# One pool of eight PSUM banks for every product, in place of three banks for dense tiles and five for the rest, with new leads

## The chip, the cores and the metric

The kernel runs on one core of a Trainium2 chip. The metric is device microseconds of one execution, as a median of several runs; less is faster. TensorE (PE in the profile) multiplies matrices and writes only to PSUM, an accumulator memory of eight banks, each of 128 partitions by 512 fp32 numbers here. VectorE (DVE) and ScalarE (ACT) read the banks and write their results to SBUF. GpSimd (POOL) helps with elementwise work in SBUF. SyncE (SP) issues all DMAs of this kernel, in order, on one queue.

## The reference

One decoder layer with 2048 prompt tokens and eight single-token samples, model width 1024:

```
h = rms_norm(x, norm_g) * (1 + scale) + shift       # scale, shift, gate from c @ w_ada
u = h @ w_in                                        # 43 tiles of 128 columns
r,k,v,wd,ad = token-shifted mix of the first 13 tiles
S  = S * w_t + sa (kk*a)^T + v_t k_t^T              # RWKV-7 state, 8 heads of 64, over time
o_a = group_norm(S r) + bonus;  y_a = o_a * silu(z_a)
o_b = window attention (128 keys back, bias, sinks); y_b = o_b * silu(z_b)
merged = sigmoid(g_a) * (y_a @ w_o_a) + sigmoid(g_b) * (y_b @ w_o_b)
y = x + gate * (merged @ w_out)
```

The outputs are y for the prompt and the samples, the recurrent states, the last shifted rows and the last 128 keys and values of each.

## The kernel before

The prompt is cut into four quarters of 512 tokens (q = 0 to 3). The samples' eight columns ride along in quarter 1, whose dense tiles are therefore 520 columns wide and are computed as two segments of 260 (`segs_of`, L836).

**Dense tiles.** Each quarter multiplies 43 tiles of `w_in`, then eight `merge` tiles (L1496) and eight `finish` tiles (L1511). The fp32 product is made of three fp32r products (high by high, high by low, low by high), so a tile takes 24 matmuls of 512 columns, or 48 of 260 in quarter 1. Each tile or segment is one accumulation in a PSUM bank of kind "d" (`pr.tile("d", ...)`), which ACT or DVE then empties (the epilogue, recorded with the lead `ELEAD`). In quarter 0 the weights are loaded whole and split into high and low parts on ACT, DVE or POOL; the parts go to DRAM and later quarters load them from there.

**Other products.** All other matmuls and transposes write banks of kind "g" (`G`, L622): the LoRA and norm sums and the pair products of the RWKV branch (`prep_pair`, L973), the 64 by 64 triangular inverses (`inverses`, L1063), the state chain of eight steps (`rwkv_group`, L1109), attention (`attend`, L1240), and the samples' work (`sample_rwkv`, L1309; `sample_attention`, L1403). The RWKV heads of a quarter form two groups of two pairs (`rwkv(0)` and `rwkv(1)`). A group keeps two "g" banks, `ops` (L1129), from its first chain step to its last. One chain step is three calls on PE with an ACT or DVE copy between them, the first of eight products, the next two of four, with four to eight more folded in (L1138 to L1159).

**The inverses** go through DRAM twice. Rows are collected from `d1` into the tile `NL`, DVE solves 31 steps, the result goes to `d2` by two DMAs (L1080) and comes back by eight more (L1088); only then can DVE transpose and PE run the 32 by 32 products (L1097).

**The order.** Python records every operation with its dependences (`Program.rec`), and `schedule` (L286) then places them one by one on modelled engines. On each engine it takes, among what could start at once, the one with the smallest priority. The priority of a dense tile is 6 times its line number; everything else gets `line * 6 - lead`, where the lead comes from the table `LEADS` (L109), with one number per kind of work, per quarter and half. `CAPS` (L108) says how many tiles of each kind exist: an operation that first writes a tile must find a free one, and must leave enough for what comes earlier in program order (`places`, L321). The kinds "d" and "g" are counted apart, three and five. The model takes a DMA as 0.45 us of SP (L423) plus its size over a rate. The order so found is written out, and each engine runs its own part strictly in that order; waits at run time come from semaphores.

Other constants touched: `HGATE` (L123) is the index of the gate tile after which the next quarter's x may load (L1632). `SWITCH` (L279) says by how much priority ACT looks past an operation that needs another activation table for one that doesn't. `NEAR` (L282) says the same for PE: while the last matmul used only a part of the array (fewer than 128 rows or columns), PE takes a ready operation of the same shape, if there is one within this much priority, ahead of the first in line (L383). `STAGES` (L127) is the program order within a quarter: "0" and "1" are the RWKV groups with their r, k and v tiles, "A" is attention with its kb, vb, q and zb tiles. After these stages come the samples' work (quarter 1 only), the za tiles, the 16 gate tiles, `merge` and `finish`. The samples' loads wait for the last dense tile recorded so far (`st["mm"][-1:]`).

Of the kernel before, what the change touches and what calls it, by code (L numbers as in the profile page):

```python
# [11 lines left out]
F32 = mybir.dt.float32  # L12
# [75 lines left out]
def _constants():  # L88
# [16 lines left out]
    one[32, ~ok] = 1.0  # L105
    return c, one, np.eye(128, dtype=np.float32)[::-1], idl

CAPS = {"p": 77, "s": 11, "t": 14, "w": 8, "nl": 1, "d": 3, "g": 5}  # L108
LEADS = {  # L109
    "prep": (2430.9, 2430.9, 2313.2, 3436.9, 452.9, 452.9, 3438.6, 3438.6),  # L110
    "inv": (2996.1, 2996.1, 5811.5, 5811.5, 5973.1, 5973.1, 5960.9, 5960.9),
    "chain": (3475.6, 3479.1, 3476.1, 3463.5, 7297.1, 3476.1, 3457.1, 3476.1),
    "gn": (2855.6, 3664.2, 3664.2, 3664.2, 3664.2, 4423.2, 2629.7, 3664.2),
    "wd": (2660.8, 2660.8, 3238.5, 3238.5, 1757.7, 1757.7, 3248.2, 3248.2),
    "norm": (4852.3, 3392.1, 820.0, 988.1, 838.5, 988.1, 838.5, 988.1),
    "att": (4680.1, 4566.4, 4726.2, 4726.2, 4352.4, 4352.4, 4902.9, 4642.8),
    "sample": (5619.9, 5482.5, 7295.5, 7295.5, 3528.3, 3528.3, 3528.3, 5619.9),
    "bias": (4326.4, 2812.3, 5008.5, 2812.3, 2812.3, 422.4, 2812.3, 2812.3),
    "h": (3270.3, 3270.3, 3270.3, 3270.3, 3270.3, 3084.9, 3270.3, 3084.9),
    "x": (390.0, 390.0, 390.0, 394.3, 390.0, 395.2, 395.2, 390.0),  # L120
}
WLEAD, ELEAD = 5000.0, 6000.0
HGATE = 3  # L123
ADA = ((0, False), (2, True), (1, False), (3, True))
EARLY, PLACE = 3, 3
INORDER = 24
STAGES = ('0A1', '01A', '0A1', '0A1')  # L127
FULL = dict(start=True, stop=True)


# [145 lines left out]
LAT, SELF_LAT = 0.2, 0.13  # L276
HELD = 0.1
DMA_LAT = 2.0
SWITCH = 10  # L279
FULL_ARRAY = (128, 128)  # L280
TURN = (0.09, 0.19)
NEAR = 8000  # L282
PE_LAT = 0.23


def schedule(prog):  # L286
# [68 lines left out]
    def pick(e):  # L355
        T = free[e]
        best = None
        for x in ready[e]:
# [8 lines left out]
            if e == "act" and o.table is not None and o.table != table[0]:  # L367
                if t <= T + 1e-9:
                    if best is None or best[0] > T + 1e-9 or False:
                        best = (t, x)  # L370
                        lim = x[0] + SWITCH
                        for y in ready[e]:
# [9 lines left out]
            if t <= T + 1e-9:  # L382
                if e == "pe" and table[1] not in (None, FULL_ARRAY, o.table[0]):  # L383
                    for y in ready[e]:
                        if y[0] > x[0] + NEAR:
                            break
# [122 lines left out]
def hybrid_step_kernel(ctx: ExitStack, tc: tile.TileContext, A, O):  # L509
# [3 lines left out]
    SQ = min(1, NQ - 1)  # L513
    caps = dict(CAPS)
    pr = Program(A["xT"].tensor, caps)
# [4 lines left out]
    psp = ctx.enter_context(tc.tile_pool(name="ps", bufs=1, space=bass.MemoryType.PSUM))  # L520
# [22 lines left out]
    def copy(out, in_, engs="act/dve"):  # L543
        do({e: "copy" if e == "act" else "tensor_copy" for e in engs.split("/")}, "copy", out, in_)
# [33 lines left out]
    def mm(out, lhsT, rhs, **k):  # L578
        pr.rec({"pe": mm_cost(out, lhsT, rhs)}, lambda e: nc.tensor.matmul(res(out), res(lhsT), res(rhs), **k), [out],  # L579
               [lhsT, rhs], table=(part(lhsT),) * 2)  # L580
# [26 lines left out]
    def dma(out, in_):  # L607
        v = [x for x in (out, in_) if isinstance(x, View)]
        shp = v[0].shape
        size = 4 * math.prod(shp)  # L610
        run = 4 * min(x.shape[-1] for x in (out, in_) if hasattr(x, "shape"))
        pr.rec({"sp": size / 359e3 * (2.0 if run < 512 else 1.0) + 0.02},
                   lambda e: nc.sync.dma_start(out=res(out), in_=res(in_)),
                   [out] if isinstance(out, View) else [], [in_] if isinstance(in_, View) else [])

    def P(shape, dt=F32):
        return pr.tile("p", shape, dt)
# [4 lines left out]
    def G(shape):  # L622
        return pr.tile("g", shape)
# [119 lines left out]
    def ada(g, whole):  # L743

        n = 9 if whole else 18
        ps = pr.tile("d", [n, 512])
        for k in range(8):
            with at(WLEAD):
                w = P([128, 512])
                with after(*st.get("mm", ())[-1:]):  # L750
                    dma(w, A["w_ada"][g, k])
                if not whole:
                    h, l = split(w)
            if whole:
                mm(ps, sc32[:, k, :], w, start=(k == 0), stop=(k == 7))
            else:
                mm(ps, sct[:, k, :], h, start=(k == 0), stop=False)
                mm(ps, sct[:, k, :], l, start=False, stop=(k == 7))
        rows = P([n, 512])
        j4 = slice(4 * g, 4 * g + 4)  # L760
        with at(ELEAD):
            copy(rows, ps)
            ps = G([128, 4, 9])
            for i in range(4):
                mm(ps[:, i, :], rows[:, 128 * i:128 * i + 128], ident[0:9, 0:9] if whole else twice, start=True, stop=True)
            add(modt[:, j4, :], ps, vc("b_ada", 4 * g, 4).unsqueeze(2).to_broadcast([128, 4, 9]))
            if g >= 4:
                ts(modt[:, j4, :], modt[:, j4, :], 0.25, None, ALU.mult)
            elif g >= 2:
                j4 = slice(4 * g - 8, 4 * g - 4)  # L770
                stt(scl[:, j4, :], modt[:, 4 * g:4 * g + 4, :], 1.0,
                    vc("norm_g", 4 * g - 8, 4).unsqueeze(2).to_broadcast([128, 4, 9]), ALU.add, ALU.mult)
        line[0] += 0.8
        pr.key = line[0] * 6.0
# [68 lines left out]
    def split(f):  # L843

        n = _free_size(f)
        h, l = P([128, n], F32R), P([128, n], F32R)
        copy(h, f)
        sub(l, f, h.f32(), "dve/pool")
        return h, l
# [61 lines left out]
    def dense(key, epi):  # L911

        wt = early.pop(key, None) or weights("w_in", INDEX[key])
        for c0, n in st["segs"]:
            ps = pr.tile("d", [128, n])
            mm3(ps, wt, range(8), st["hk"], c0, n)
            m = min(c0 + n, CH) - c0
            with at(ELEAD):
                epi(ps[:, 0:m], c0, m)
                if c0 + n > CH:  # L920
                    copy(st["us"][:, INDEX[key], :], ps[:, m:n])
        step_line()
# [562 lines left out]
    def gated(key):  # L1485
        t = P([128, W if len(st["segs"]) > 1 else CH])
        wt = weights("w_in", INDEX[key])
        for c0, n in st["segs"]:
            ps = pr.tile("d", [128, n])
            mm3(ps, wt, range(8), st["hk"], c0, n)  # L1490
            with at(ELEAD):
                act(t[:, c0:c0 + n], ps, AF.Tanh, scale=0.5)
        step_line()
        return t

    def merge(j, ga, gb, ya, yb, segs):  # L1496
        wo = weights("w_o", j)
        for c0, n in segs:
            cols = slice(c0, c0 + n)
            for x, t, ks in ((gb, yb, slice(4, 8)), (ga, ya, slice(0, 4))):  # L1500
                ps = pr.tile("d", [128, n])
                mm3(ps, (wo[0][:, ks, :], wo[1][:, ks, :]), range(4), t, c0, n)
                with at(ELEAD):
                    stt(x[:, cols], x[:, cols], 1.0, ps, ALU.add, ALU.mult)
        with at(ELEAD):
            add(ga, ga, gb, "dve/pool")
            m = split(ga)
        step_line()
        return m

    def finish(q, j, ms, segs):  # L1511
        sample = q == SQ
        xt = P([128, CH])
        with at(LEAD["x"]), after(*st["mm"][-3:-2]):
            dma(xt, A["xT"][j, :, q * CH:(q + 1) * CH])
        wt = weights("w_out", j)
        for c0, n in segs:
            ps = pr.tile("d", [128, n])
            mm3(ps, wt, range(8), ms, c0, n)
            m = min(c0 + n, CH) - c0  # L1520
            with at(ELEAD):
                stt(xt[:, c0:c0 + m], ps[:, 0:m], modt[:, 16 + j, 0:1], xt[:, c0:c0 + m], ALU.mult, ALU.add)
                if c0 + n > CH:
                    t = Sm([128, NB])
                    mul(t, ps[:, m:n], modt[:, 16 + j, 1:9])
                    add(t, t, st["xst"][:, j, :])
                    dma(O["ysT"][:, j, :], t)
        with at(ELEAD):
            dma(O["yT"][j, :, q * CH:(q + 1) * CH], xt)
        step_line()  # L1530
# [10 lines left out]
    for q in range(NQ):  # L1541
        sample = q == SQ
        w = W if sample else CH
# [4 lines left out]
        x = shifted(("wd", 0))  # L1548
# [50 lines left out]

        for stage in STAGES[min(q, 3)]:  # L1600
            if stage == "A":
# [28 lines left out]
        for j in range(8):  # L1630
            gates.append((gated(("ga", j)), gated(("gb", j))))
            if j == HGATE:  # L1632
                st["gate"] = (st["mm"][-1],)
# [10 lines left out]

    order = schedule(pr)
    size = {"p": 520, "s": 128, "t": 16, "w": 1024, "nl": 1024}
    banks = {k: [psp.tile([128, 512], F32, name=f"{k}{i}") for i in range(caps[k])] for k in "dg"}
    made = set()
    with tc.manual_schedule():
        for o in order:  # L1650
            for b in o.born:
                if b not in made:
                    made.add(b)
                    k, i = b.kind, b.place
                    b.place = banks[k][i] if k in banks else work.tile([128, size[k]], b.dtype, tag=f"{k}{i}",
                                                                       name=f"{k}{i}_{len(made)}")
# [75 lines left out]
```

## Time and profile before

| | |
|---|---|
| runs: 1878.34, 1876.17, 1885.71 us | median 1878.34 us |
| the profiled execution | 1877.38 us, of which the span of the trace is 1875.6 us |
| PE matmul busy | 1794.4 us, 96% of the span |
| PE weight load (beside the matmuls) | 1438.6 us |
| DVE, ACT, POOL busy | 1290.4, 789.9, 115.8 us |
| DMA | 343.19 MB, mean 183 GB/s, 53.4% of the 16 engines |
| mean granted clock of TensorE | 0.990 |

In the profile, a group such as "d<-p,w" names the tile that is written and the tiles that are read; "d" is a dense bank, "g" one of the others, "p" a work tile in SBUF, "w" a weight tile. Nearly all DVE, ACT and POOL operations carry the line L538, that of the helper that emits them, so the tile names tell them apart. Matmuls of dense tiles, transforms with `blocks` and the ada products are at L579, calls of several products at L597, transposes at L604. An fp32 product (not fp32r) shows as two records. "idle before" is the time for which the engine had nothing running, with what released it; "issue" stands where the profile shows no releaser.

### The profile page before, as it was taken

To read this page: it belongs to the slowest core of one execution; us is meant where nothing else is said; L and a number is where in the kernel's file an instruction comes from. 1 tells how busy PE (TensorE), PEld (TensorE's weight loads), DVE (VectorE), ACT (ScalarE), POOL (GpSimd) and SP (SyncE) were. 2 spreads that over 40 slices of the span, in tenths; PEclk is the share of its full clock that TensorE was granted. 3 is DMA by queue.
4 is the path that set the end of the run, shared out by engine and by line. 5 is a ranking of instruction groups with operands and counts; after the bars stand their busy time and mean duration, and the time that the engine had idled before them with its cause. 6 is when DMAs were issued, how large, how long until landed. Compare 5 with 4: busy or idle time off the path is not lost.

```text
span 1875.6 us, 32659 instructions
## 1 busy us (share of the span) xinstructions
PE 1794.4 (96%) x12544; PEld 1438.6 (77%) x12544; DVE 1290.4 (69%) x3110; ACT 789.9 (42%) x1608; POOL 115.8 (6%) x187
## 2 busy tenths in 40 slices
PE   6999999999999999799999999999999999999999
PEld 2767666777799989688998787677678777678787
DVE  7889979567378968388534886876452887776261
ACT  5667555442155544256103554723301663551300
POOL 0000220000001210000000100100000000110000
PEclk9999999999999999799999999999999999999999
DMA  9475537837855355234566464257267455236355
GB/s 357 171 260 213 175 130 279 306 136 288 308 174 174 125 164 163 86 119 151 188 233 209 136 203 141 68 167 228 89 228 259 150 187 162 91 113 195 112 197 184
DMA packets 162455, 343.19 MB, mean 183 GB/s; under 512 B 65485, under 2 KB 69246, under 8 KB 162300
## 3 DMA queue, kind: packets, MB, share of 16 engines
q1 hardware_dynamic: 162300, 341.11, 53.4%
q8 instruction: 99, 1.62, 0.4%
q14 instruction: 56, 0.46, 0.1%
HBM read 263.09 MB, written 77.96 MB: 182 GB/s over the span
## 4 chain that ended last, share of the span: by engine, by line
PE 49%; DVE 16%; ACT 4%; DMA 3%; issue 1%; POOL 0%; SPq 0%; DVEq 0%; ACTq 0%; POOLq 0%
PE d L579 40%; DVE p L538 16%; PE g L597 5%; ACT p L538 3%; PE g L579 2%; PE g L604 1%; ACT L538 1%; DMA p<-d 1%; DMA d<-p 1%; DMA p<-in_lora 0%; DMA p<-in_xT 0%; DVE t L538 0%; DVE s L538 0%; DMA w<-lo_w_in 0%; POOL p L538 0%
## 5 line engine op out<-in xcount | busy, mean ns | idle before, releaser
L579 PE MATMUL d<-p,w 128*128 128x512 f32 (+1 forms) x7080 | 1450.2, 355 | 18.5 <-DVE w L538 10.7
L579 PEld LDWEIGHTS d<-p,w 128*128 128x128 f32 x7080 | 1137.4, 189 | 217.3 <-DVE w L538 17.4
L538 DVE TENSOR_TENSOR p<-p,p 128x512 fp32r<-128x512 f32 (+6 forms) x573 | 348.8, 631 | 43.0 <-ACT p L538 32.3
L597 PE MATMUL g<-p,p 128*64 128x64 f32 (+5 forms) x4000 | 228.5, 243 | 20.7 <-DVE p L538 18.6
L597 PEld LDWEIGHTS g<-p,p 128*64 128x64 f32 (+4 forms) x4000 | 177.1, 142 | 86.6 <-DVE p L538 30.6
L538 ACT COPY p<-g 64x128 f32<-64x128 f32 (+3 forms) x362 | 131.4, 373 | 133.9 <-PE g L597 77.3
L538 ACT ACTIVATE p<-d 128x512 f32<-128x512 f32 (+1 forms) x120 | 61.0, 512 | 216.9 <-PE d L579 168.5
L538 ACT CAST p<-p 128x512 fp32r<-128x512 f32 (+2 forms) x176 | 106.1, 617 | 101.5 <-DVE p L538 94.8
L538 ACT ACT_TABLE_LOAD x105 | 134.7, 1283 | 21.5 <-PE g L579 17.7
L538 ACT ACTIVATE p<-d,vec 128x511 f32<-128x511 f32 (+1 forms) x65 | 38.9, 602 | 230.1 <-PE d L579 227.1
L538 DVE TENSOR_TENSOR p<-p,nl 128x2 f32<-128x2 f32 (+30 forms) x248 | 127.0, 512 | 12.4 <-DMA p<-in_idl 7.4
L538 DVE SCALAR_TENSOR_TENSOR p<-p,d 128x512 f32<-128x512 f32 (+1 forms) x120 | 69.4, 580 | 70.9 <-PE d L579 70.0
L538 DVE TENSOR_TENSOR p<-g,s 64x128 f32<-64x128 f32 (+1 forms) x124 | 40.2, 326 | 101.2 <-PE g L597 95.1
L538 DVE SCALAR_TENSOR_TENSOR p<-d,modt,p 128x512 f32<-128x512 f32 (+2 forms) x40 | 25.7, 643 | 120.7 <-PE d L579 115.9
L538 ACT ACTIVATE p<-p 128x512 f32<-128x512 f32 (+2 forms) x161 | 98.3, 633 | 24.0 <-DMA p<-in_xT 12.8
L538 ACT CAST w<-w 128x1024 fp32r<-128x1024 f32 x59 | 61.8, 1049 | 90.1 <-PE d L579 43.7
L538 DVE TENSOR_TENSOR w<-w,w 128x1024 fp32r<-128x1024 f32 x58 | 70.8, 1221 | 39.7 <-PE d L579 32.0
L579 PE MATMUL g<-p,blocks 128*128 128x512 f32 x204 | 81.3, 433 | 14.1 <-DVE p L538 8.8
L538 POOL TENSOR_TENSOR p<-p,p 64x256 f32<-64x256 f32 (+2 forms) x52 | 62.3, 1213 | 513.3 <-DVE p L538 259.0
L538 DVE TENSOR_REDUCE p<-p 128x1 f32<-128x2 f32 (+31 forms) x252 | 89.1, 354 | 4.7
L538 DVE TENSOR_TENSOR p<-g,cst 64x256 f32<-64x256 f32 (+1 forms) x192 | 88.2, 507 | 3.2 <-PE g L597 2.3
L604 PE MATMUL g<-cst,p 128*128 128x128 f32 (+1 forms) x457 | 71.3, 277 | 5.3 <-DVE p L538 3.4
(146 smaller groups left out, 1056.8 us busy)
## 6 DMA issues: line engine op xcount, KB each, us to landing
w<-hi_w_in SPq DMA_DIRECT2D x129, 512.0 KB, 3.7
w<-lo_w_in SPq DMA_DIRECT2D x129, 512.0 KB, 4.6
w<-in_w_in SPq DMA_DIRECT2D x43, 512.0 KB, 5.8
hi_w_in<-w SPq DMA_DIRECT2D x43, 512.0 KB, 3.7
lo_w_in<-w SPq DMA_DIRECT2D x43, 512.0 KB, 4.1
p<-in_xT SPq DMA_DIRECT2D x64, 256.0 KB, 6.0
p<-in_w_ada SPq DMA_DIRECT2D x48, 256.0 KB, 5.3
w<-hi_w_o SPq DMA_DIRECT2D x24, 512.0 KB, 3.6
```

Source lines behind the costliest of these rows:

```text
L538: lambda e: getattr(ENG[e], engs[e])(res(out), *(res(x) for x in a), **{n_: res(v) for n_, v in k.items()}),
L579: pr.rec({"pe": mm_cost(out, lhsT, rhs)}, lambda e: nc.tensor.matmul(res(out), res(lhsT), res(rhs), **k), [out], [lhsT, rhs], table=(part( ...
L597: nc.tensor.matmul(res(out), res(lhsT), res(rhs), **k)
L604: pr.rec({"pe": 2 * _free_size(in_) / 2400.0 + 0.003}, lambda e: nc.tensor.transpose(res(out), res(in_), res(idn)), [out], [in_, idn], tab ...
```

## The change

The kinds "d" and "g" become one kind "g" with eight banks: every `pr.tile("d", ...)` asks for "g", so a dense tile may take any bank, and so may any other product. The leads, the program order of quarter 1 (attention now between its two RWKV groups, as in the other quarters) and three constants get other values. No operation is added or removed, and no size changes.

```diff
-CAPS = {"p": 77, "s": 11, "t": 14, "w": 8, "nl": 1, "d": 3, "g": 5}
+CAPS = {"p": 77, "s": 11, "t": 14, "w": 8, "nl": 1, "g": 8}
 LEADS = {
-    "prep": (2430.9, 2430.9, 2313.2, 3436.9, 452.9, 452.9, 3438.6, 3438.6),
-    "inv": (2996.1, 2996.1, 5811.5, 5811.5, 5973.1, 5973.1, 5960.9, 5960.9),
-    "chain": (3475.6, 3479.1, 3476.1, 3463.5, 7297.1, 3476.1, 3457.1, 3476.1),
+    "prep": (2430.9, 2615.8, 2615.8, 1827.7, 2615.8, 2615.8, 2615.8, 2615.8),
+    "inv": (2996.1, 2378.5, 2378.5, 2378.5, 2378.5, 3849.7, 2378.5, 3849.7),
+    "chain": (2171.2, 2171.2, 2171.2, 3837.4, 2171.2, 2171.2, 3457.1, 2171.2),
...
-    "att": (4680.1, 4566.4, 4726.2, 4726.2, 4352.4, 4352.4, 4902.9, 4642.8),
-    "sample": (5619.9, 5482.5, 7295.5, 7295.5, 3528.3, 3528.3, 3528.3, 5619.9),
+    "att": (4680.1, 4566.4, 4726.2, 4726.2, 4252.8, 5882.4, 4280.7, 4280.7),
+    "sample": (5619.9, 5482.5, 7295.5, 7295.5, 3528.3, 3528.3, 3535.3, 3540.9),
...
-HGATE = 3
+HGATE = 1
...
-STAGES = ('0A1', '01A', '0A1', '0A1')
+STAGES = ('0A1', '0A1', '0A1', '0A1')
...
-SWITCH = 10
+SWITCH = 3
...
-NEAR = 8000
+NEAR = 0
...
-            ps = pr.tile("d", [128, n])
+            ps = pr.tile("g", [128, n])
```

The last pair of lines stands for the tiles of `dense`, `gated`, `merge`, `finish` and `ada`; the banks are then made from whichever of the two kinds the table has.

More of the change, by code (lines that the diff above doesn't have):

```diff
@@ L106, in _constants @@
     return c, one, np.eye(128, dtype=np.float32)[::-1], idl
-CAPS = {"p": 77, "s": 11, "t": 14, "w": 8, "nl": 1, "d": 3, "g": 5}
+CAPS = {"p": 77, "s": 11, "t": 14, "w": 8, "nl": 1, "g": 8}
 LEADS = {
-    "prep": (2430.9, 2430.9, 2313.2, 3436.9, 452.9, 452.9, 3438.6, 3438.6),
-    "inv": (2996.1, 2996.1, 5811.5, 5811.5, 5973.1, 5973.1, 5960.9, 5960.9),
-    "chain": (3475.6, 3479.1, 3476.1, 3463.5, 7297.1, 3476.1, 3457.1, 3476.1),
-    "gn": (2855.6, 3664.2, 3664.2, 3664.2, 3664.2, 4423.2, 2629.7, 3664.2),
-    "wd": (2660.8, 2660.8, 3238.5, 3238.5, 1757.7, 1757.7, 3248.2, 3248.2),
-    "norm": (4852.3, 3392.1, 820.0, 988.1, 838.5, 988.1, 838.5, 988.1),
-    "att": (4680.1, 4566.4, 4726.2, 4726.2, 4352.4, 4352.4, 4902.9, 4642.8),
-    "sample": (5619.9, 5482.5, 7295.5, 7295.5, 3528.3, 3528.3, 3528.3, 5619.9),
-    "bias": (4326.4, 2812.3, 5008.5, 2812.3, 2812.3, 422.4, 2812.3, 2812.3),
-    "h": (3270.3, 3270.3, 3270.3, 3270.3, 3270.3, 3084.9, 3270.3, 3084.9),
-    "x": (390.0, 390.0, 390.0, 394.3, 390.0, 395.2, 395.2, 390.0),
+    "prep": (2430.9, 2615.8, 2615.8, 1827.7, 2615.8, 2615.8, 2615.8, 2615.8),
+    "inv": (2996.1, 2378.5, 2378.5, 2378.5, 2378.5, 3849.7, 2378.5, 3849.7),
+    "chain": (2171.2, 2171.2, 2171.2, 3837.4, 2171.2, 2171.2, 3457.1, 2171.2),
+    "gn": (2855.6, 3664.2, 3311.7, 3311.7, 4662.5, 5678.9, 2629.7, 5678.9),
+    "wd": (2660.8, 2660.8, 3238.5, 1687.1, 1002.5, 1757.7, 1002.5, 3248.2),
+    "norm": (2988.6, 2988.6, 3981.8, 2988.6, 2988.6, 988.1, 2988.6, 2872.9),
+    "att": (4680.1, 4566.4, 4726.2, 4726.2, 4252.8, 5882.4, 4280.7, 4280.7),
+    "sample": (5619.9, 5482.5, 7295.5, 7295.5, 3528.3, 3528.3, 3535.3, 3540.9),
+    "bias": (4326.4, 2812.3, 5008.5, 1534.4, 1568.4, 422.4, 786.0, 786.0),
+    "h": (3162.4, 3270.3, 3162.4, 3162.4, 3162.4, 3138.4, 3162.4, 3392.0),
+    "x": (375.3, 396.3, 374.9, 374.9, 390.0, 396.3, 396.3, 396.3),
 }
 WLEAD, ELEAD = 5000.0, 6000.0
-HGATE = 3
+HGATE = 1
 ADA = ((0, False), (2, True), (1, False), (3, True))
@@ L745, in ada @@
         n = 9 if whole else 18
-        ps = pr.tile("d", [n, 512])
+        ps = pr.tile("g", [n, 512])
         for k in range(8):
@@ L1488, in gated @@
         for c0, n in st["segs"]:
-            ps = pr.tile("d", [128, n])
+            ps = pr.tile("g", [128, n])
             mm3(ps, wt, range(8), st["hk"], c0, n)
@@ L1500, in merge @@
             for x, t, ks in ((gb, yb, slice(4, 8)), (ga, ya, slice(0, 4))):
-                ps = pr.tile("d", [128, n])
+                ps = pr.tile("g", [128, n])
                 mm3(ps, (wo[0][:, ks, :], wo[1][:, ks, :]), range(4), t, c0, n)
@@ L1517, in finish @@
         for c0, n in segs:
-            ps = pr.tile("d", [128, n])
+            ps = pr.tile("g", [128, n])
             mm3(ps, wt, range(8), ms, c0, n)
@@ L1646, in hybrid_step_kernel @@
     size = {"p": 520, "s": 128, "t": 16, "w": 1024, "nl": 1024}
-    banks = {k: [psp.tile([128, 512], F32, name=f"{k}{i}") for i in range(caps[k])] for k in "dg"}
+    banks = {k: [psp.tile([128, 512], F32, name=f"{k}{i}") for i in range(caps[k])] for k in caps if k in "dg"}
     made = set()
```

## The prediction

> **What bounds the kernel now.** I read the page first, then the list of who waited for whom on PE, then the chain of waits in order of time, then timelines and windows around the longest waits. The page:
>
> ```profile
> span 1875.6 us, 32659 instructions
> ...
> PE 1794.4 (96%) x12544; PEld 1438.6 (77%) x12544; DVE 1290.4 (69%) x3110; ACT 789.9 (42%) x1608; POOL 115.8 (6%) x187
> ...
> L579 PE MATMUL d<-p,w 128*128 128x512 f32 (+1 forms) x7080 | 1450.2, 355 | 18.5 <-DVE w L538 10.7
> ```
>
> PE is the bound: it is busy in all but 81 us of the span. The change removes no matmul, so it can win only from those 81 us, from clock that was not granted, and from the cost of turning PE from one shape of product to another. The waits of PE (engine, line, who released it: us in total, times, longest):
>
> ```profile
> PE g L597 <- DVE p L538: 18.6, 11, 12.4
> PE d L579 <- ACT p L538: 13.8, 2, 13.6
> PE d L579 <- DVE w L538: 10.7, 15, 1.4
> PE g L579 <- DVE p L538: 9.3, 17, 1.7
> PE g L579 <- ACT p L538: 5.2, 9, 1.1
> PE g L604 <- DVE p L538: 3.4, 6, 1.1
> PE d L579 <- DVE p L538: 3.3, 4, 1.6
> PE d L579 <- issue: 2.3, 1, 2.3
> ```
>
> Two single waits stand out. The 13.6 us is the start of the program: the first operands must be loaded and split, and the change leaves that alone. The 12.4 us is one wait in quarter 1. The 10.7 us are weights of quarter 0 that DVE has not yet split; no bank plays a part in them. The chain of waits (start, us, what) gives the two rates of dense tiles at their best, and what lies in the 12.4 us:
>
> ```profile
> 740.25 9.00 DMA d<-p
> 749.34 12.30 DMA p<-d
> ...
> 882.12 131.20 PE d L579 x1055
> ...
> 1776.15 95.32 PE d L579 x410
> ```
>
> A matmul of 260 columns takes 131.20/1055 = 0.124 us, one of 512 columns 95.32/410 = 0.2325 us. Both stretches are free of waits, so more banks can give nothing there.
>
> **Part 1: dense tiles that waited for a bank.** Timelines of DVE and PE around the three longest waits of a dense matmul for an epilogue (start, us, engine; idle before it in brackets):
>
> ```profile
> 579.52 0.88 DVE L538 SCALAR_TENSOR_TENSOR p<-d,omm,p 128x260 f32<-128x260 f32 x2
> 580.06 1.02 PEld L579 LDWEIGHTS d<-p,w 128*128 128x128 f32 x8 [1.80 <-DVE p L538]
> 580.06 1.10 PE L579 MATMUL d<-p,w 128*128 128x260 f32 x7 [1.59 <-DVE p L538]
> ...
> 1637.95 0.47 PE L579 MATMUL d<-p,w 128*128 128x512 f32 x1 [2.27 <-issue]
> ...
> 1361.26 0.96 PE L579 MATMUL d<-p,w 128*128 128x512 f32 x3 [1.16 <-DVE p L538]
> ```
>
> At 580 the dense product starts while DVE is emptying dense banks that it had left standing behind pair products: with three banks, the fourth tile cannot begin. I read the other two in the same way. Together they are 1.59 + 2.27 + 1.16 = 5.0 us. In a pool of eight a dense tile finds a bank unless the other work holds the rest; a group's chain holds two for long. I take all 5.0 us as gained. The bounds are 0 (the chain, attention and preparation hold the banks, so that the wait only changes its name) and 5.6 us, the two last rows of the list of waits. What is late next behind such a wait is only the next tile; the epilogue that DVE was late with stays late, and that costs nothing while another bank is free.
>
> **Part 2: the 12.4 us of quarter 1 and the clock after it.** Windows around it (length, busy time of each engine with its count, granted clock, DMA share, GB/s):
>
> ```profile
> 749.00:753.00 4.00, 0.79 (x7) 0.58 (x5) 0.00 (x0) 0.00 (x0) 0.00 (x0) 1.00 0.25 100
> 753.00:762.00 9.00, 0.00 (x0) 0.00 (x0) 0.34 (x1) 0.00 (x0) 0.00 (x0) 0.53 0.22 48
> 762.00:774.00 12.00, 11.70 (x171) 10.86 (x172) 3.43 (x10) 3.86 (x10) 0.00 (x0) 0.50 0.34 106
> 774.00:780.00 6.00, 6.00 (x81) 5.00 (x79) 0.87 (x3) 1.31 (x5) 0.40 (x1) 1.00 0.38 150
> ```
>
> PE stops at about 749.8, and so do DVE, ACT and POOL: all stand behind the round trip of an inverse through DRAM. Dense tiles are queued on PE behind the 32 by 32 products that need it, and PE keeps its order. From about 753 the clock is halved, and it stays so until 774, 12 us after PE resumed. PE is 11.70 us busy there at half clock, work of 5.9 us, so the halving costs 5.9 us more. Why was this trip late? The SP queue before it, and the usual times to landing:
>
> ```profile
> 728.26 5.77 SPq L613 DMA_DIRECT2D out_kws<-p  x1
> 734.12 2.35 SPq L613 DMA_DIRECT2D w<-hi_w_in  x1
> ...
> 739.66 4.52 SPq L613 DMA_DIRECT2D d<-p  x2
> ```
>
> ```profile
> d<-p SPq DMA_DIRECT2D x16, 128.0 KB, 3.1
> p<-d SPq DMA_DIRECT2D x64, 32.0 KB, 4.1
> ```
>
> The two DMAs to `d2` took 9.0 us where 3.1 is the median, and the way back 12.3 where one takes 4.1. Just before, SP spent 5.77 us on the samples' `out_kws`, where the order counts 0.45. In the old quarter 1 the samples' work begins after the attention tiles, which come last, and by then the second group's inverse is running: both meet on SP. In the new order the second group's r, k and v come after attention. The samples' loads wait for the last of those tiles, so `out_kws` follows it closely, while that group's inverse must first go through preparation, `d1`, `NL` and 31 steps on DVE. So the meeting goes away, and I take 12.4 + 5.9 = 18.3 us as gained. The bounds are 18.3 and 0, since seven other round trips remain that a new order can make late. The PE work that stood behind the wait is dense, and the waiting call is passed later or met in time.
>
> The Trainium skill, "TensorE: Matmul & The Clock Gate", "Part 1: The HAM clock gate", says that an idle window of about 3.4 us halves the clock, and that about 3.4 us of sustained work restores it. The fall fits, some 4 us after PE stopped; the return took 12 us here, with PE 11.70 of 12.00 us busy. By the page the half clock would cost an estimated 1.7 us and the forecast would be 1860.
>
> **Part 3: turns of PE, and `NEAR`.** One step of a chain among dense tiles of 260 columns:
>
> ```profile
> 775.92 1.10 PE L579 MATMUL d<-p,w 128*128 128x260 f32 x7
> 776.96 0.69 PE L597 MATMUL g<-p,p 128*64 128x64 f32 x16
> 777.57 0.75 PE L579 MATMUL d<-p,w 128*128 128x260 f32 x4
> 778.25 0.45 PE L597 MATMUL g<-s,p 64*64 64x64 f32 x8
> 778.53 0.40 PE L597 MATMUL g<-p,p 64*64 64x64 f32 x8
> 778.86 0.87 PE L579 MATMUL d<-p,w 128*128 128x260 f32 x5
> 779.65 0.45 PE L597 MATMUL g<-p,p 128*64 128x64 f32 x8
> ```
>
> From start to start the 16 dense matmuls take 1.04 + 0.68 + 0.79 = 2.51 us, against 16 x 0.124 = 1.98: an excursion to smaller products costs the dense side 0.53/3 = 0.18 us. Eight groups of eight steps with three calls are 192 excursions if none are joined, some 35 us. `NEAR` = 8000 tries to join calls of one shape, and 0 gives that up. But the rows show each call of a step alone between dense tiles: it waits for a copy of the call before, so there was little to join. If a fifth of the 192 had been joined, their loss would cost 38 x 0.18 = 7 us; if a chain's call starts sooner because it need not stand behind a like one, the most there is to win is one 0.69 us call now and then. I take 1 us of loss, near the second bound because of those rows.
>
> The Trainium skill, "TensorEngine Tiling (Array Packing)", "Key Properties", says that a change of tiling mode drains TensorE. It speaks against `NEAR` = 0 wherever calls had been joined, has no figure, and the 0.18 us agrees with it.
>
> **Part 4: edits costed at nothing.** The other waits for "g" products (12.4 us taken off) are 6.2 + 9.3 + 5.2 + 3.4 = 24.1 us in the rows above, mostly about 0.6 us each, for an operand that DVE or ACT has just split, not for a bank. New leads deal them anew: between 24.1 us won and as much lost, I take 0. `SWITCH` concerns ACT, 42% busy, hidden by PE. `HGATE` = 1 starts x loads two gate pairs earlier, into the wait-free stretches above; if they came too early they would only hold SBUF tiles. The inverse falls from above attention and weights to below them in every quarter but 0; that is slack which I count as a rival.
>
> **The sum.** 1877.4 (the profiled execution's own time) - 5.0 - 12.4 - 5.9 + 1.0 = 1855.1. The median of the runs, 1878.3, is 1.0 above that execution, so the forecast is 1856 us, 1.2% less.
>
> **Rivals.** (a) The late trip moves: another inverse meets a burst on SP, and 18.3 us come back: 1874. For it: SP carries every DMA, and the order counts 0.45 us where SP took 5.77 and 4.52. Against it: seven of eight trips did not stop PE for long. 25%.
>
> (b) Slower: the second group becomes the tail of quarter 1. It is supported by these rows (the memset opens the eighth inverse's solve, the `blocks` product is the group norm's; then quarters 1 and 2 before their wait-free stretch):
>
> ```profile
> L538 DVE MEMSET nl<- x8: 85/85/85, 130.8 to 1684.8; 128x32 f32 x8
> ...
> L579 PE MATMUL g<-p,blocks x204: 208/397/796, 14.8 to 1775.8; 128*128 128x512 f32 x100, 128*128 128x8 f32 x1, 128*128 128x32 f32 x1
> ...
> 469.00:882.00 413.00, 386.26 (x3406) 347.28 (x3406) 299.09 (x781) 188.72 (x431) 39.59 (x54) 0.97 0.49 162
> ...
> 1013.00:1364.00 351.00, 341.13 (x2360) 260.84 (x2358) 254.36 (x648) 167.33 (x348) 23.45 (x33) 1.00 0.45 145
> ```
>
> In quarter 3, which already has this order, the second group needs 91 us from 1684.8 to 1775.8, and the wait-free stretch begins at 1776.15: filler and group end together. Quarter 1 has 299 - 254 = 45 us more DVE work, the samples', at high priority, and only 20 x (48 x 0.124 - 24 x 0.2325) = 7.5 us more filler in its 20 za and gate tiles. If all 45 us fell into the group's way, PE would stand 37.5 us before the merges and pay 5.9 for the clock: 1856 + 43 = 1899. It makes the kernel slower once PE stands about 26 us there. Against it: that DVE work can be done while the group waits for its round trip. 12%.
>
> (c) More: the pool lets preparation, chain and attention overlap, and half of the 24.1 us go: 1844. 10%.
>
> (d) The change doesn't do what it says, since dense tiles seldom lacked a bank, and small waits of new places outweigh the gains: 1877 to 1895. 8%.
>
> The forecast itself, 1845 to 1868, has 45%. A difference under 0.5% (9.4 us) can't be told from no change here, so faster means below 1869 and slower above 1888. Faster: 45 + 10 + 2 of (a) = 57%. Same: 23 of (a) and 4 of (d) = 27%. Slower: 12 and 4 of (d) = 16%. The range from 1840 to 1888 leaves out (b), half of (d) and a part of (c), about 2 in 10.
>
> **What would show it.** In the new profile no wait of PE for a 32 by 32 product should be over 2 us, and the mean clock should rise from 0.990 towards 0.995. The rows "d <- DVE p" and "d <- issue" should fall from 5.6 us to under 2. Starts from dense to dense around a chain should keep the 0.18 us. I am wrong if PE stands over 10 us anywhere but at the start, above all before the merges of quarter 1, or if the waits for "g" products leave the span of 12 to 36 us.

## The result and the profile after

The changed kernel takes 1857.84 us, the median of six runs from 1855.46 to 1861.22; the kernel before, run beside it, takes 1877.26. The ratio is 0.989, with a 95% interval from 0.988 to 0.991. The profiled execution took 1855.46 us, with a span of 1853.3. The page's rows for the bound:

```profile
span 1853.3 us, 32547 instructions
...
PE 1786.4 (96%) x12544; PEld 1430.8 (77%) x12544; DVE 1292.0 (70%) x3128; ACT 783.3 (42%) x1612; POOL 88.6 (5%) x163
```

PE has the same 12544 matmuls. Its idle time in the span fell from 81.2 to 66.9 us, by 14.3, and its busy time by 8.0: together the 22.3 us that the span lost. The view of spans and granted clocks says more of the 8.0:

```profile
core 0: 1853.3 us, clock 0.997
```

Before, the mean clock was 0.990. What a halved clock costs is half the time for which PE is busy under it, as the prediction reckoned for its one stretch. The kernel before has three more such stretches; windows around the first and the last of them (length, busy time of each engine, granted clock, DMA share, GB/s):

```profile
367.00:378.00 11.00, 11.00 (x75) 7.26 (x70) 4.95 (x12) 4.83 (x8) 0.40 (x1) 0.54 0.64 259
...
818.00:822.00 4.00, 4.00 (x19) 3.61 (x18) 3.62 (x8) 1.08 (x2) 0.00 (x0) 0.57 0.00 0
```

In the two traces PE is busy at half clock for 28.8 us before and 7.9 us after. That is 14.4 and 3.9 us of work not done, 10.5 less, while PE's busy time fell by 8.0. Some 2.5 us of PE time therefore came in elsewhere; the runs give no cause for it, and the reckoning assumes that every product takes twice as long at half clock. The waits of PE, in which dense tiles and other products now share the name "g":

```profile
PE g L579 <- ACT p L538: 19.2, 12, 13.6
PE g L579 <- DVE p L538: 12.9, 18, 6.6
...
PE g L597 <- DVE p L538: 4.1, 10, 0.7
```

The 13.6 us of the start stands as before. The wait of 12.4 us for 32 by 32 products (L597) is gone, and no such call waits over 0.7 us. But one wait of 6.6 us is new. Windows, then SP's timeline and the chain of waits around it:

```profile
740.00:747.50 7.50, 7.50 (x60) 6.16 (x60) 5.02 (x17) 3.72 (x12) 0.00 (x0) 1.00 0.43 136
747.50:754.00 6.50, 0.23 (x2) 0.02 (x1) 0.15 (x2) 0.88 (x2) 0.00 (x0) 0.84 0.50 136
754.00:758.00 4.00, 3.71 (x14) 3.43 (x15) 3.94 (x8) 1.31 (x2) 1.66 (x1) 0.50 0.13 50
```

```profile
721.00 0.40 SPq L613 DMA_DIRECT2D out_kws<-p  x1
...
722.06 4.33 SPq L613 DMA_DIRECT2D out_kws<-p  x1
726.44 2.55 SPq L613 DMA_DIRECT2D out_vws<-p  x1
732.05 5.23 SPq L613 DMA_DIRECT2D w<-hi_w_in  x1
...
737.96 5.13 SPq L613 DMA_DIRECT2D d<-p  x4
...
749.37 1.13 SPq L613 DMA_DIRECT2D nl<-d  x2
```

```profile
741.79 7.43 DMA d<-p
```

The samples' transfers and the second group's inverse still meet on SP. They now meet on the inverse's first trip, through `d1`, not on its second, through `d2`: the writes to `d1` take 7.4 us, DVE stands at the memset of `NL`, and PE stands behind DVE. Quarter 1 does not wait before its merges.

### The profile page after: what moved, and what is told of

It is laid out like the page before. It is cut to its first block, busy times and chain, and to the rows that moved or that the text cites. A ratio compares the mean times of both kernels' runs of the same rounds, so it can differ in the third digit from the quotient of the medians.

```text
span 1853.3 us, 32547 instructions
## 1 busy us (share of the span) xinstructions
PE 1786.4 (96%) x12544; PEld 1430.8 (77%) x12544; DVE 1292.0 (70%) x3128; ACT 783.3 (42%) x1612; POOL 88.6 (5%) x163
## 4 chain that ended last, share of the span: by engine, by line
PE 59%; DVE 16%; ACT 3%; DMA 2%; issue 1%; SPq 0%; DVEq 0%; ACTq 0%
PE g L579 52%; DVE p L538 15%; PE g L597 6%; ACT p L538 2%; PE g L604 1%; ACT L538 1%; DMA p<-d 1%; DMA d<-p 1%; SPq L613 0%; DMA p<-in_xT 0%; DVE s L538 0%; DVE w L538 0%; DVE t L538 0%; DMA lo_w_out<-w 0%; DMA nl<-d 0%
## 5 line engine op out<-in xcount | busy, mean ns | idle before, releaser
L579 PE MATMUL g<-p,w 128*128 128x512 f32 (+1 forms) x7080 | 1442.4, 354 | 16.8 <-DVE w L538 8.4
L579 PEld LDWEIGHTS g<-p,w 128*128 128x128 f32 x7080 | 1135.8, 188 | 215.9 <-DVE w L538 13.8
L538 DVE TENSOR_TENSOR p<-p,p 128x512 fp32r<-128x512 f32 (+5 forms) x596 | 354.7, 617 | 45.6 <-ACT p L538 28.7
L597 PE MATMUL g<-p,p 128*64 128x64 f32 (+6 forms) x4000 | 224.2, 240 | 5.6 <-DVE p L538 4.1
L597 PEld LDWEIGHTS g<-p,p 128*64 128x64 f32 (+4 forms) x4000 | 172.0, 140 | 70.4 <-ACT p L538 21.8
L538 ACT COPY p<-g 64x128 f32<-64x128 f32 (+5 forms) x410 | 147.2, 370 | 162.8 <-PE g L597 69.9
L538 ACT ACTIVATE p<-g 128x512 f32<-128x512 f32 (+2 forms) x136 | 70.4, 523 | 167.8 <-PE g L579 146.5
L538 ACT CAST p<-p 128x512 fp32r<-128x512 f32 (+3 forms) x167 | 99.8, 610 | 92.0 <-DVE p L538 87.6
L538 DVE SCALAR_TENSOR_TENSOR p<-p,g 128x512 f32<-128x512 f32 (+1 forms) x120 | 69.4, 579 | 91.5 <-PE g L579 89.8
L538 DVE TENSOR_REDUCE p<-p 128x5 f32<-128x50 f32 (+30 forms) x252 | 89.0, 354 | 4.7
L538 DVE CAST p<-p 128x512 fp32r<-128x512 f32 (+4 forms) x140 | 58.2, 420 | 23.0 <-ACT p L538 13.8
```

The source lines that it names most:

```text
L538: lambda e: getattr(ENG[e], engs[e])(res(out), *(res(x) for x in a), **{n_: res(v) for n_, v in k.items()}),
```

## The experiments

Ratios are to the kernel before, run on the same chip; the changed kernel's is 0.989. They go in three steps: what made the trip late, what the pool does alone, and what the new order is worth.

**The trip and SP's queue.** First the kernel before, in its own order, without the four transfers.

```diff
-            o.emit(o.on)
+            if o not in st["skip"]:      # the out_kws and out_vws of whole windows
+                o.emit(o.on)
```

> The kernel before, its order kept on every engine, without the four large transfers of the samples' shifted key and value windows to the outputs (out_kws and out_vws: these outputs are left out). Theory (the samples' transfers made the inverse's round trip late on SP): the two writes to d2 land in about 3 to 5 us instead of 9.0, the way back takes 4 to 7, PE's wait of 12.4 us falls under 4 us, the halved clock from 753 to 774 goes, and the time falls by 14 to 18 us, to about 1860. Rival 1 (the weight loads on SP or the 128-byte pieces of the trip itself make it late): the wait stays over 9 us and the time stays within 5 us of before. Rival 2 (the trip is early now but PE's order runs into the next late operand): the wait falls, the time falls by less than 8 us.

It took 1861.85 us, ratio 0.991 (0.987 to 0.994), 16.4 us less than the kernel before beside it. SP's timeline, the chain and the waits of PE:

```profile
738.01 1.26 SPq L613 DMA_DIRECT2D d<-p  x2
```

```profile
739.24 8.90 PE d L579 x73
748.14 1.13 PE g L597 x64
```

```profile
PE g L597 <- DVE p L538: 7.0, 13, 2.5
```

The two writes to `d2` now occupy SP for 1.26 us where it had been 4.52, and PE goes from 73 dense matmuls to the 32 by 32 products without a wait. So the four transfers are the cause, as part 2 of the prediction said, at 16.4 us where it had 18.3.

Next the changed kernel, with the four transfers moved behind the loads of `NL` on SP.

```diff
     order = schedule(pr)
+    # on SP, the four transfers go behind the NL loads of quarter 1's second group
+    for o in late[::-1]:
+        order.insert(j, order.pop(i))
```

> The changed kernel, its order kept on every engine except that on SP the four large transfers of the samples' key and value windows to the outputs go behind the two loads of NL of the same quarter's second group. Theory (the meeting on SP only moved from the way through d2 to the way through d1, and left 6.6 us of wait and 10.2 us of halved clock): the wait at 754 falls under 2 us, the clock stays at 1.00 there, and the time falls by 6 to 11 us against the changed kernel, to a ratio of about 0.985 to before. Rival (the writes to d1 and the weight loads before them are late by themselves): the wait stays over 4 us and the ratio stays at 0.989.

It took 1868.83 us, ratio 0.995 (0.993 to 0.997): worse than the changed kernel. SP's timeline, and the timelines of ACT and DVE where PE waited:

```profile
741.29 1.13 SPq L613 DMA_DIRECT2D nl<-d  x2
742.46 0.45 SPq L613 DMA_DIRECT2D out_vws<-p  x1
742.96 4.43 SPq L613 DMA_DIRECT2D out_kws<-p  x1
747.43 2.44 SPq L613 DMA_DIRECT2D out_vws<-p  x1
749.92 8.06 SPq L613 DMA_DIRECT2D out_kws<-p  x1
758.02 2.51 SPq L613 DMA_DIRECT2D p<-in_swkv  x1
```

```profile
756.44 0.59 ACT L538 COPY p<-g 128x512 f32<-128x512 f32 x1 [7.05 <-DMA out_kws<-p]
...
768.01 0.69 DVE L538 TENSOR_TENSOR p<-p,s 128x512 f32<-128x512 f32 x1 [10.02 <-DMA p<-in_swkv]
```

The loads of `NL` went out 8 us sooner, as the theory said, but the expectation of the time failed. The four transfers hold SP for 0.45 + 4.43 + 2.44 + 8.06 = 15.4 us there, against 7.6 in the changed kernel. PE waited twice: 6.5 us because ACT stood until an `out_kws` had read the tile that ACT was to write, and 8.1 us because DVE stood for the samples' state (`in_swkv`), whose load was now behind the four.

So the last of these runs leaves the order alone and takes the transfers off SP.

```diff
-            dma(O["kws"][:, b4, :], kc[j][:, :, 1:129])
+            dma(O["kws"][:, b4, :], kc[j][:, :, 1:129], "gpsimd")   # nc.gpsimd.dma_start
...
-            dma(O["vws"][0:127, b4, :], vcache[j][1:128])
+            dma(O["vws"][0:127, b4, :], vcache[j][1:128], "gpsimd")
```

> The changed kernel, its order kept, with the four large transfers of the samples' key and value windows issued by GpSimd on its own queue in place of SP. Theory (these transfers hold up SP's queue by some 12 to 15 us, and whatever stands behind them there is late: the trip through d1 in the changed kernel, through d2 in the one before): the wait of 6.6 us falls under 2 us, the clock is no longer halved around it, and the ratio to before falls from 0.989 to 0.982 to 0.986. Rival 1 (the 16 DMA engines, not the queue, are held up): the wait stays over 4 us, ratio 0.988 to 0.990. Rival 2 (GpSimd stands behind its transfers, and DVE behind GpSimd): ratio 0.990 or more.

It took 1848.69 us, ratio 0.985 (0.983 to 0.987): faster than both kernels. Its spans and clock, its waits, and POOL's timeline:

```profile
core 0: 1845.6 us, clock 1.000
```

```profile
PE g L579 <- DVE p L538: 7.8, 19, 0.9
```

```profile
721.93 0.92 POOL L613 DMA_DIRECT2D out_kws<-p  x1 [5.90 <-DVE s L538]
...
723.59 0.58 POOL L613 DMA_DIRECT2D out_vws<-p  x1
724.16 0.77 POOL L613 DMA_DIRECT2D out_kws<-p  x1
724.93 0.56 POOL L613 DMA_DIRECT2D out_vws<-p  x1
```

The wait of 6.6 us has gone, and this execution shows no loss of clock at all (0.995 to 0.998 in the other four). Issuing the four costs POOL 0.92 + 0.58 + 0.77 + 0.56 = 2.8 us. The same edit in the kernel before:

> The kernel before, its order kept, with the four large transfers of the samples' key and value windows issued by GpSimd on its own queue; nothing is left out. Theory (the SP queue was the matter, as when the transfers were left out): 1860 to 1864, ratio to before 0.990 to 0.993, no wait of PE for 32 by 32 products over 4 us. Then the changed kernel with the same queue, at 0.985, is some 0.6% ahead by its order alone. Rival (the transfers themselves, not their queue, were in the way): ratio 0.996 or more.

It took 1862.87 us, ratio 0.992 (0.989 to 0.994), like the run that left the transfers out. So what was in the way is how these transfers go out from SP, and not that they are made.

What they do there can be read in a window of the changed kernel in which SP stands for 5.23 us at a weight load, beside one of the run with GpSimd's queue in which all four go out:

```profile
734.00:737.00 3.00, 2.27 (x19) 2.06 (x19) 2.97 (x8) 0.59 (x1) 2.00 (x2) 1.00 0.07 27
```

```profile
722.00:728.00 6.00, 5.38 (x62) 4.62 (x63) 5.76 (x15) 3.95 (x8) 4.76 (x8) 1.00 0.62 178
```

A DMA share of 0.07 is about one of the 16 DMA engines. The packets in the trace there have 2048 bytes, the size of a row of `out_vws`, and go out one after another, 12 or 13 a microsecond, so that one `out_vws` (127 rows, 254 KB) takes some 10 us on one engine. What SP issues behind it has a part on that engine too. Of the 1024 pieces of 128 bytes that the changed kernel writes to `d1`, 960 had started by 743.9; the other 64, one in sixteen, started at 748.0 to 748.6. In the kernel before it was 128 of the 2048 pieces for `d2`, and the second `out_vws` lay over the way back, from 751 to 761. From GpSimd's queue the four go in packets of 4096 bytes, and several engines share them. So one DMA engine of the queue was held up, not all 16. No run parts the two `out_vws` from the two `out_kws`, or leaves them on SP and spreads them there.

The Trainium skill, "DMA: Bandwidth & Descriptors", "Issuing engines are not separate DMA queues", says that starting DMAs from several engines saves only the sequencer's time, which it calls usually small beside the DMA itself. Here that time was 5.77 us of SP for one `out_kws` before, and taking it off SP was worth 18 us in the kernel before and some 8 in the changed one (0.989 to 0.985); but as the packets changed with the queue, these runs do not show the sequencer's time by itself.

**The pool by itself.** The kernel before, with its order, and the banks dealt anew after planning:

```diff
-    banks = {k: [psp.tile(...) for i in range(caps[k])] for k in "dg"}
+    banks = [psp.tile([128, 512], F32, name=f"b{i}") for i in range(8)]
+    # after planning: each product takes the bank that has been empty longest
```

> The kernel before with its order kept on every engine; only the banks are dealt anew after planning, each product taking that of all eight which has been empty longest. This is the pool without new leads and without a new order. Theory: the three waits of dense tiles for a bank (1.6, 2.3 and 1.2 us) go, little else moves, 1871 to 1875, ratio 0.996 to 0.999, and the wait of 12.4 us stays. Rival 1 (banks stood behind many of the small waits too): ratio under 0.994. Rival 2 (those waits change their name but stay, since DVE is late for the next thing as well): ratio 0.999 to 1.001.

It took 1876.08 us over twelve runs, ratio 0.9992 (0.9978 to 1.0006): no change, and at most 4 us, as rival 2 had it. Its waits, and timelines where the three waits of part 1 had been ("b" is any bank):

```profile
PE b L597 <- DVE p L538: 19.2, 10, 12.3
```

```profile
571.81 5.07 PE L579 MATMUL b<-p,w 128*128 128x260 f32 x41
576.80 0.49 PE L597 MATMUL b<-p,p 64*128 64x128 f32 x2
578.46 2.02 PE L597 MATMUL b<-p,p 64*128 64x128 f32 x30 [1.17 <-DVE p L538]
...
1359.01 0.62 ACT L538 CAST p<-p 128x512 fp32r<-128x512 f32 x1 [4.15 <-DVE p L538]
1359.68 1.51 PE L579 MATMUL b<-p,w 128*128 128x512 f32 x4 [1.62 <-ACT p L538]
...
1632.88 0.75 DVE L538 SCALAR_TENSOR_TENSOR p<-b,omm,p 128x512 f32<-128x512 f32 x1
1633.73 0.48 PE L579 MATMUL b<-p,w 128*128 128x512 f32 x1 [2.25 <-issue]
```

In the kernel before, the second and the third wait had ended 0.06 and 0.10 us after DVE had emptied a dense bank:

```profile
1360.52 0.68 DVE L538 SCALAR_TENSOR_TENSOR p<-p,d 128x512 f32<-128x512 f32 x1
...
1637.10 0.75 DVE L538 SCALAR_TENSOR_TENSOR p<-d,omm,p 128x512 f32<-128x512 f32 x1
```

In the order of the kernel before, these banks are the ones that the waiting tiles take, so all three waits were for a bank. With the banks dealt anew, the first (1.59 us) is gone and the dense tile runs on, but the next call, a pair product, waits 1.17 us for DVE, which is as late as ever. The second (1.16 us) is gone from its place, but six matmuls later PE stands 1.62 us, where it had been 0.20, for an operand that ACT is still splitting. The third stays: the tile again starts 0.10 us after DVE has emptied a dense bank, and the dealing gives it just that bank. A larger pool was no help there.

Now the pool in the planner, with the old leads, program order and constants, and the other way round, the changed kernel with three and five banks:

```diff
-CAPS = {"p": 77, "s": 11, "t": 14, "w": 8, "nl": 1, "d": 3, "g": 5}
+CAPS = {"p": 77, "s": 11, "t": 14, "w": 8, "nl": 1, "g": 8}
```

> The kernel before with one pool of eight banks and nothing else changed (old leads, program order and constants). Theory (the pool removes the waits of dense tiles for a bank, 5 us, and the late round trip is the matter of the program order): 1870 to 1874, ratio 0.997, no wait of a dense matmul for a dense epilogue over 0.5 us, and a wait of about 12 us for 32 by 32 products of quarter 1 still there. Rival 1 (the pool is what makes the order better): ratio 0.990 or less. Rival 2 (the old leads fit only three and five): slower than before, ratio over 1.003.

> The changed kernel with three banks for dense tiles and five for the rest again, everything else as changed. Theory (the pool is worth about 5 us of 20, the rest is program order): ratio to before 0.991 to 0.994, and dense matmuls wait for dense epilogues again, 3 to 6 us in all. Rival 1 (the pool carries the gain): ratio 0.998 or more. Rival 2 (the pool carries nothing): 0.989.

The first took 1914.54 us, ratio 1.019 (1.015 to 1.022); the second 1913.69, ratio 1.018 (1.015 to 1.021). The theory failed for both; rival 2 of the first and rival 1 of the second came. Waits of the second:

```profile
PE g L597 <- DVE p L538: 37.9, 15, 14.1
```

Its order calls for 32 by 32 products long before DVE has solved their inverse: three times PE stands 8.8 to 14.1 us. To take the meeting on SP out of it, both were run again with the four transfers on GpSimd's queue:

> The kernel before with the pool of eight and old leads, and with the four transfers on GpSimd's queue. Theory (the pool with old leads makes an order with many waits that have nothing to do with these transfers): ratio to before 1.005 to 1.015, several waits of PE over 2 us remain. Rival (its loss was the meeting on SP alone): 0.995 or less.

> The changed kernel with three and five banks again, and with the four transfers on GpSimd's queue. Theory (the new leads need the pool: DVE comes late with solves of the inverse that PE's order has already called for): ratio to before 1.008 to 1.018, waits of 8 to 14 us for 32 by 32 products remain. Rival (its loss was the meeting on SP): 0.995 or less.

1907.35 us, ratio 1.016 (1.012 to 1.019), and 1908.33 us, ratio 1.014 (1.011 to 1.017). With that queue there are then four kernels: old leads with three and five banks 0.992, old leads with the pool 1.016, new leads, order and constants with three and five banks 1.014, and with the pool 0.985. Neither half is worth anything without the other.

**The program order of quarter 1, alone and put back.**

```diff
-STAGES = ('0A1', '01A', '0A1', '0A1')
+STAGES = ('0A1', '0A1', '0A1', '0A1')
```

> The kernel before with only the program order of quarter 1 changed (attention between its two RWKV groups); old leads, three and five banks. Theory (program order moves the inverse away from the samples' transfers): no wait over 8 us for the round trip through d2 in quarter 1, ratio 0.990 to 0.994. Rival 1 (another trip or the trip through d1 is late instead): ratio 0.995 to 1.005. Rival 2 (as with the pool alone, an edit without its leads makes a worse order): ratio over 1.005.

> The changed kernel with only the program order of quarter 1 put back (both RWKV groups before attention). Theory: a round trip through d2 meets the samples' transfers again and PE waits 8 to 15 us there, ratio 0.996 to 1.002. Rival 1 (the order of quarter 1 does not matter): 0.988 to 0.991. Rival 2 (leads and program order fit only each other): over 1.005, with more than one late trip.

Alone it took 1888.25 us, ratio 1.006 (1.004 to 1.008), with a wait of 10.1 us for another inverse and 5.6 us for split operands later in the quarter, so that neither half of the theory held. Put back in the changed kernel it took 1912.02 us, ratio 1.019 (1.016 to 1.022). The waits of the latter, and windows at the longest:

```profile
PE g L597 <- DVE p L538: 48.8, 21, 27.0
```

```profile
760.00:774.00 14.00, 0.53 (x5) 0.32 (x3) 13.24 (x30) 0.00 (x0) 0.00 (x0) 0.68 0.31 105
774.00:787.00 13.00, 0.00 (x0) 0.00 (x0) 7.80 (x12) 0.00 (x0) 0.30 (x1) 0.50 0.37 108
```

DVE is solving alone (13.24 of 14 us) while PE stands for 27.0 us with dense tiles behind the call. So it is an early call in PE's order more than a late DMA.

**`NEAR` back to 8000** in the changed kernel with GpSimd's queue:

```diff
-NEAR = 0
+NEAR = 8000
```

> The changed kernel with NEAR at 8000 as before, and with the four transfers on GpSimd's queue; to be held against the changed kernel with that queue (ratio 0.985). Theory (there is little to join, so the order hardly changes): fewer than 15 excursions of PE are joined, ratio 0.983 to 0.988. Rival (any edit of the planner deals a new order with its own late calls): ratio over 0.990, with a wait of PE over 5 us that the other does not have.

It took 1863.16 us, ratio 0.991 (0.989 to 0.993), against 0.985. Counted in the records of matmuls, PE turns 531 times between array shapes against 536, so five turns were saved, 0.45 us at 0.18 us an excursion of two turns. PE's timeline and the clock show where the 0.6% went:

```profile
327.62 0.22 PE L597 MATMUL g<-p,p 32*32 32x32 f32 x2 [3.16 <-DVE p L538]
332.12 1.06 PE L597 MATMUL g<-p,p 32*32 32x32 f32 x30 [4.28 <-DVE p L538]
336.70 0.31 PE L597 MATMUL g<-p,p 32*32 32x32 f32 x2 [3.53 <-DVE p L538]
```

```profile
core 0: 1860.7 us, clock 0.991
```

The planner drew the calls of one inverse together, and PE stood 3.16 + 4.28 + 3.53 = 11.0 us between them with no dense tile in between. Against the profile with `NEAR` = 0 the span is 15.1 us longer: 6.7 us are idle time of PE, and 8.4 us are busy time, at a clock of 0.991 against 1.000. The ratio is the rival's, though no wait but that of the start is over 4.3 us. The theory was right on the turns and wrong on the time. `SWITCH` and `HGATE` were not tried.

## Why the prediction was right, and where not

The forecast was 1856 us and the median is 1858. The medians of the two kernels, run beside each other, are 19.4 us apart; the spans of the two profiles are 22.3 us apart, which is what the sum said, though the profile after is of the fastest of its six runs. So close a hit was luck in good part, for the terms were not that good.

The runs on GpSimd's queue split the gain in two. Without the meeting on SP the kernel before is at 0.992 and the changed one at 0.985, so the new order is worth some 12 us, for which the sum had nothing. The meeting costs the kernel before 16 to 18 us and still costs the changed one some 8, so 8 to 10 us came from there, for which the sum had 18.3.

- **What bounds the kernel** held: the gain is idle time of PE and clock, nothing else.
- **Part 1, 5.0 us for dense tiles that waited for a bank**: the reading was right, and all three waits were for a bank. The step that failed is "I take all 5.0 us as gained". What was late next behind such a wait was not "only the next tile" but an operand from DVE or ACT, so that in the old order the time stayed the same within 4 us, near the bound of 0 that the step named. In the changed kernel the waits of dense tiles for anything but weights fell from 5.6 to 1.6 us, but those for weights rose from 12.8 to 14.6.
- **Part 2, the cause of the 12.4 us**, was right as to the four transfers: without them on SP it is gone, for 16 us by one run and 18 by the other, against the 18.3 that the sum gave to it. It pointed at the 5.77 us of SP for an `out_kws`; the traces point at the `out_vws`, on one DMA engine, and no run parts the two. The step that failed is "So the meeting goes away". The inverse's way through `d2` is free, but the prediction names `d1` among what comes before it and does not count that the way through `d1` is on SP too. There it met the transfers, and 6.6 us of the wait came back. This is rival (a) in kind, though on another way of the same inverse, and at some 8 us less than half of its price. The sum had 12.4 us of wait here; the change has 5.8.
- **The halved clock**: 5.9 us was right for the one stretch that it was worked out for, but in all 10.5 us came off. Of the other three stretches one fell after a wait of 2.35 us, one after waits of 1.07 and 0.59 us, and one with no wait over 0.11 us in the 10 us before it, so the waits alone do not say where the clock halves.
- **Part 3, turns**: 1.0 us of loss. The 0.18 us stands (16 dense matmuls around a chain step take 2.52 us in the changed kernel, against 2.51), and setting `NEAR` back saved only five turns, so there was little to join, as it said. But the constant moves the time through the order, by 0.6% and the other way, which the bounds (7 us of loss, 0.69 us of win at a time) did not hold.
- **Part 4, leads at 0**, was the largest mistake, hidden by the others. The old leads with the pool lose 1.9%, the new ones without it 1.8%. The 12 us of the new order belong to leads, pool, program order and constants together: with `NEAR` alone put back nearly all of them are gone (0.991). In the profiles with GpSimd's queue the span falls by 14.0 us from the old order to the new one; 6.6 us of it are idle time of PE and 7.4 us busy time, at a clock of 0.994 before and 1.000 after.
- **Rival (b)** did not come: PE does not stand before the merges of quarter 1. Rivals (c) and (d) did not come as priced; but what (c) said of the small waits is in part what the new order did.

So the errors cancelled: idle time fell by 14.3 us where 17.4 were forecast, the clock gave 10.5 where it was 5.9, and 2.5 us of PE time came in where 1.0 was counted. Of the idle time, 5.8 us come from the meeting, some 7 from small waits of products other than dense tiles and some 2 from dense tiles; waits too short to be listed took back 1. The signs that the prediction named all came: no wait for a 32 by 32 product is over 0.7 us, the clock is 0.997 (0.992 to 0.996 in the other runs), PE stands over 10 us only at the start, and the waits for other products, without the start and the 6.6 us, are 24.2 us.

Of the rule quoted from the Trainium skill, "TensorE: Matmul & The Clock Gate", "Part 1: The HAM clock gate": after the new wait of the changed kernel, PE resumes at 754.3; the clock is 0.50 up to 758 in the window shown above and 0.95 in the next one, below, so it is back at about 758.8. The return took some 4.5 us, nearer to the 3.4 of the Trainium skill than the 12 us seen in the trace of before.

```profile
758.00:766.00 8.00, 8.00 (x61) 7.78 (x61) 7.35 (x18) 7.16 (x12) 0.00 (x0) 0.95 0.41 149
```

## What to carry to other kernels

In an order written out ahead, one call that stands too early on the bounding engine can cost far more than the resource that the edit is about: such calls cost up to 27.0 us here, every half of this change, tried alone, lost 0.6 to 1.9%, and the banks themselves, in the old order, were worth nothing that could be measured. Before a gain is put down to a buffer, deal out the buffers anew in the same order and look whether the wait goes or only moves to the next late operand. And a few transfers that hold up the one queue that carries everything belong on another engine's queue: here four DMAs moved to GpSimd gave some 8 us on top of the change.

## What was not expected of the hardware

Four output transfers of about 256 KB held SP for up to 8.06 us each when others stood before them in the queue, where the first of a batch took 0.40 us; GpSimd issued each in under 1 us. Two of them, of 127 rows each, went out on one of the 16 DMA engines from SP's queue, at 25 GB/s, and over several engines from GpSimd's. In the changed kernel the `out_kws` landed in a median of 3.6 us from GpSimd where it had been 8.0 from SP; in the kernel before, where SP had issued them 8 us apart, it was 5.3 against 4.8, so GpSimd's queue is not faster by itself:

```profile
out_kws<-p SPq DMA_DIRECT2D x2, 256.0 KB, 8.0
```

```profile
out_kws<-p POOLq DMA_DIRECT2D x2, 256.0 KB, 3.6
```
